# Scores of the stick-breaking and memory heads from 64 rows each, in place of zero-padded 128 rows

## The chip, the cores and the metric

One core of one Trainium2 chip runs the whole program: two blocks of a transformer on 512 tokens of 1024 features. The metric is the device time of one execution in microseconds (us), the median over several runs. The engines are named as the profile names them: PE (TensorE, matrix products), PEld (its weight loads), DVE (VectorE), ACT (ScalarE), POOL (GpSimd) and SP (SyncE, which issues most DMAs).

## The reference, cut to what matters

The first block mixes three kinds of heads (8 stick-breaking heads, 4 heads of a gated recurrence called HGRN, 4 memory heads), adds the result to `x`, and then runs a mixture of experts (PEER). The second block has dilated-window heads and again 4 memory heads. All heads that matter here have 64 features.

```python
def stick_breaking_attention(q, k, v):
    ...
        z = jnp.einsum('bhqd,bhkd->bhqk', q_blk, kh).astype(jnp.float32) * scale
        mask = key_pos[None, :] < q_pos[:, None]
        log_1m = jnp.where(mask, jax.nn.log_sigmoid(-z), 0.0)
        tail = lax.cumsum(log_1m, axis=3, reverse=True) - log_1m
        log_a = jax.nn.log_sigmoid(z) + tail
        a = jnp.where(mask, jnp.exp(log_a), 0.0)
        return jnp.einsum('bhqk,bhkd->bhqd', a.astype(vh.dtype), vh)
...
def memory_attention(q, mem_k, mem_v, q_gain, k_gain):
    qn = rms_norm(q, q_gain)
    kn = rms_norm(mem_k, k_gain)
    logits = jnp.einsum('bshd,bmhd->bhsm', qn, kn).astype(jnp.float32) * scale
    p = jax.nn.softmax(logits, axis=-1)
    return jnp.einsum('bhsm,bmhd->bshd', p.astype(mem_v.dtype), mem_v)
```

The scores `z` and `logits` are sums over only 64 features per head.

## The kernel before, in words

The code is a Tile program: the author writes operations on tiles of named pools, and a scheduler sets the order in which each engine gets its instructions. A pool with two buffers under one name hands them out in the order in which the code asks for them, so the third tile of that name waits until the first is free.

**First block, mixer.** `feat` and `tok` project the normalised tokens with a slab of weights (`mm_feat`, L115 to L123, with 128x512 results; `mm_tok`, L125 to L133, with 128x256 results). Each weight slab is loaded by SP and split into a high part by ACT (L107) and a low part by POOL (L108). These projections depend on little and serve as filler on PE between the pieces of the head computations. The calls at L563 to L582 set the priority: `stick_in(0)`, `stick(0)`, `hgrn_in(0)`, `hgrn(0)`, `stick_in(1)`, `hgrn(1)`, `stick(1)`, `hgrn_in(1)`, `hgrn(2)`, `hgrn(3)`, then `tok` 11 and 12, `mem_q`, `mem_kv`, `mem_out`. After them come `hgrn_out`, the transposes of the mixed rows and the output projection.

**Heads in pairs.** 128 partitions hold the features of two heads: the lower head in rows 0 to 63, the upper one in rows 64 to 127. The queries are kept twice, once with the upper rows zero and once with the lower rows zero (`zero_pads`, L235 to L238, sets the zeros; `padded`, L228 to L233, writes the two halves), so that a product over all 128 rows gives the scores of one head.

**`stick`** (L281) handles four heads at once. For every block of 128 queries (`qb`) it goes through the key blocks `kb` from `qb` down to 0, ten pairs of blocks in all. For each pair:

```python
pz = psa.tile([P, 512], F32, name="att")
for i in range(2):
    nc.tensor.matmul(pz[:, i * 256:(i + 1) * 256], kT[:, i, kb * P:(kb + 1) * P],
                     qz[:, i, :, qb * P:(qb + 1) * P], start=True, stop=True)
z = pool.tile([P, 512], F32, name="sb_a", bufs=4)
...
pc = psa.tile([P, 512], F32, name="att")
```

Both `pz` (scores) and `pc` (cumulative sums) come from `att`, which has two PSUM banks in the first block. DVE copies `pz` to `z` (L297, L299), three ACT passes and one DVE pass make a softplus (L301 to L304), ACT and DVE split it (`sh` L307, `sl` L308), PE sums it into `pc` (L310 with `sh`, L311 with `sl`, L313 with those of earlier blocks), DVE subtracts (L315), ACT takes the exponential (L316). At the end of a query block PE multiplies with the values (L321).

**`hgrn_head`** (L328) runs one recurrence head through eight rounds of DVE, ACT, DVE, PE (scores, L346) and DVE, and ends with the products at L384 to L388.

**`mem_attn`** (L240) serves both blocks: per 128 tokens four score products of 128x256 (L250), two in a bank; maximum (L253), exponentials (L258), transposes (L268), values (L276). In the second block `fill` puts projections between its pieces, and it takes its queries from the tile `dw_qz`, which the window heads use before it (`featT(9, qz, 0.125)`, L1028).

Products with f32 operands appear in the trace as two records (a weight load and a product each) per instruction; products with fp32r operands as one.

Of the kernel before, what the change touches and what calls it, by code (L numbers as in the profile page):

```python
# [84 lines left out]
class Body:  # L85
# [154 lines left out]
    def mem_attn(self, qz, kT, v, emit, pool, psa, pst, psm, scale, fill=None):  # L240

        nc = self.nc
        for b in range(NB):
            p = [pool.tile([P, 2, 256], F32, name="ma_a", bufs=2) for _ in range(2)]
            sm = pool.tile([P, 4], F32, name="ma_sm", bufs=2)
            mx = pool.tile([P, 4], F32, name="ma_mx", bufs=2)
            for c in range(2):
                ps = psa.tile([P, 512], F32, name="att")
                for j in range(2):
                    nc.tensor.matmul(ps[:, j * 256:(j + 1) * 256], qz[:, c, j, b * P:(b + 1) * P], kT[:, c, :],  # L250
                                     start=True, stop=True)
                m = mx[:, 2 * c:2 * c + 2]
                nc.vector.tensor_reduce(m, ps.rearrange("p (j m) -> p j m", j=2), axis=AX.X, op=OP.max, negate=True)  # L253
                if scale != 1.0:
                    nc.vector.tensor_scalar(m, m, scale, None, op0=OP.mult)
                for j in range(2):
                    h = 2 * c + j
                    nc.scalar.activation(p[c][:, j, :], ps[:, j * 256:(j + 1) * 256], AF.Exp, bias=mx[:, h:h + 1],  # L258
                                         scale=scale, accum_out=sm[:, h:h + 1])
# [21 lines left out]
    def stick(self, g, qz, kT, v, mixed, pool, psa, pso):  # L281

        nc = self.nc
        bc = lambda m: m[:, None, :].to_broadcast([P, 4, P])
        v4 = lambda t: t.rearrange("p (h q) -> p h q", h=4)
        for qb in range(NB):
            po = pso.tile([P, 512], F32, name="acc")
            at, parts = {}, []
            for kb in range(qb, -1, -1):
                pz = psa.tile([P, 512], F32, name="att")  # L290
                for i in range(2):
                    nc.tensor.matmul(pz[:, i * 256:(i + 1) * 256], kT[:, i, kb * P:(kb + 1) * P],
                                     qz[:, i, :, qb * P:(qb + 1) * P], start=True, stop=True)

                z = pool.tile([P, 512], F32, name="sb_a", bufs=4)
                if kb == qb:
                    nc.vector.tensor_tensor(v4(z), v4(pz), bc(self.mneg), op=OP.add)  # L297
                else:
                    nc.vector.tensor_copy(z, pz)  # L299
                sp = pool.tile([P, 512], F32, name="sb_sp", bufs=2)  # L300
                nc.scalar.activation(sp, z, AF.Abs)  # L301
                nc.scalar.activation(sp, sp, AF.Exp, scale=-1.0)
                nc.scalar.activation(sp, sp, AF.Ln, bias=1.0)
                nc.vector.scalar_tensor_tensor(sp, z, 0.0, sp, op0=OP.max, op1=OP.add)  # L304
# [10 lines left out]
                nc.vector.tensor_tensor(z, z, pc, op=OP.subtract)  # L315
                nc.scalar.activation(z, z, AF.Exp)  # L316
                at[kb] = z
            for h in range(4):
                c = h // 2
                for kb in range(qb, -1, -1):  # L320
                    nc.tensor.matmul(po[:, h * P:(h + 1) * P], at[kb][:, h * P:(h + 1) * P],  # L321
                                     v[:, kb, c * P:(c + 1) * P], start=kb == qb, stop=kb == 0)
# [105 lines left out]
    def first(self, cp, gp, xr):  # L428
        nc, tc, A = self.nc, self.tc, self.A
        with ExitStack() as es:  # L430
# [84 lines left out]
            def stick_in(eng, g):  # L515
                qz = tp.tile([P, 2, 2, S], F32, name="sb_qz", bufs=2)
                kT = tp.tile([P, 2, S], F32, name="sb_kT", bufs=2)
                v = tp.tile([P, NB, 256], F32, name="sb_v", bufs=2)
                self.zero_pads(qz, eng)
                feat(g, qz, 0.125)  # L520
                feat(2 + g, kT)
                tok(4 + g, slabs(v))
                return qz, kT, v
# [7 lines left out]
            def mem_q():  # L531
                mqz = tp.tile([P, 2, 2, S], F32, name="sb_qz", bufs=2)
                self.zero_pads(mqz, nc.gpsimd)
# [4 lines left out]
                for c in range(2):  # L538
# [3 lines left out]
                    self.padded(mqz[:, c], ps, self.vec[:, V_MQ:V_MQ + 1])  # L542
# [21 lines left out]
            sb = stick_in(nc.vector, 0)  # L564
# [5 lines left out]
            sb = stick_in(nc.gpsimd, 1)  # L570
# [329 lines left out]
    def second(self):  # L900
        nc, tc, A = self.nc, self.tc, self.A
        with ExitStack() as es:
# [125 lines left out]
            featT(9, qz, 0.125)  # L1028
# [28 lines left out]
            self.mem_attn(qz, kTm, vm, emit, pool, psa, pst, psm, 1.0, fill)  # L1057
# [113 lines left out]
```

## Time and profile before

| what | value |
|---|---|
| median of 3 runs | 2064.39 us (2060.55 to 2064.94) |
| the profiled execution, its own time | 2068.49 us |
| its span in the profile | 2066.7 us |
| PE busy | 1940.7 us, 94% of the span |
| DVE busy | 1428.8 us, 69% |
| ACT busy | 886.0 us, 43% |
| POOL busy | 639.8 us, 31% |
| score products of `stick` (L292) | 80 records, 21.8 us busy |
| score products of `mem_attn` (L250), first and second block | 32 and 32 records, 9.9 and 8.6 us busy |

Read it by stages: the mixer of the first block runs from 0 to about 405 us, the experts to about 1750 us, the second block to the end. Busy times of PE overlap, since products are pipelined: the time from the start of one record to the start of the next tells what a record costs, and it is shorter than its duration.

### The profile page before, as it was taken

To read this page: it belongs to the slowest core of one execution; us is meant where nothing else is said; L and a number is where in the kernel's file an instruction comes from. 1 tells how busy PE (TensorE), PEld (TensorE's weight loads), DVE (VectorE), ACT (ScalarE), POOL (GpSimd) and SP (SyncE) were. 2 spreads that over 40 slices of the span, in tenths; PEclk is the share of its full clock that TensorE was granted. 3 is DMA by queue.
4 is the path that set the end of the run, shared out by engine and by line. 5 is a ranking of instruction groups with operands and counts; after the bars stand their busy time and mean duration, and the time that the engine had idled before them with its cause. 6 is when DMAs were issued, how large, how long until landed. Compare 5 with 4: busy or idle time off the path is not lost.

```text
span 2066.7 us, 30059 instructions
## 1 busy us (share of the span) xinstructions
PE 1940.7 (94%) x11393; PEld 1760.8 (85%) x11393; DVE 1428.8 (69%) x2662; ACT 886.0 (43%) x1373; POOL 639.8 (31%) x459
## 2 busy tenths in 40 slices
PE   7999988998779999999999999999999999999998
PEld 6778777998779899899999999999999777779998
DVE  3486976379998866778777777877778675443563
ACT  4564745254437666333333333333333334343352
POOL 4334233075452230144333434343333341000000
PEclk9999999999899999999999999999999999999999
DMA  4211014354224445999888988988988775342211
GB/s 163 69 62 50 33 42 143 123 164 133 92 92 180 177 163 222 313 314 335 304 306 308 316 310 284 337 315 302 313 297 291 272 270 196 103 136 74 82 62 52
DMA packets 150354, 402.90 MB, mean 195 GB/s; under 512 B 11584, under 2 KB 60736, under 8 KB 147008
## 3 DMA queue, kind: packets, MB, share of 16 engines
q1 hardware_dynamic: 112768, 264.64, 38.2%
q0 software_dynamic: 36864, 134.23, 18.0%
q8 instruction: 89, 1.46, 0.3%
q10 hardware_dynamic: 576, 2.10, 0.3%
q14 instruction: 57, 0.47, 0.1%
HBM read 371.05 MB, written 29.88 MB: 194 GB/s over the span
## 4 chain that ended last, share of the span: by engine, by line
PE 59%; DVE 12%; DMA 5%; issue 3%; POOL 1%; ACT 1%; DVEq 0%; POOLq 0%; ACTq 0%
PE o L679 21%; PE hp L634 7%; PE hp L633 7%; PE hp L632 7%; DMA g_row<-peer_v,idx 3%; PE mm L121 2%; PE mm L122 2%; PE mm L123 2%; PE mm L133 2%; PE mm L132 2%; PE mm L131 2%; DVE gated L854 1%; PE g L860 1%; PE mm L861 1%; PE g L861 1%
## 5 line engine op out<-in xcount | busy, mean ns | idle before, releaser
L107 ACT ACTIVATE w_hi<-w_raw 128x1024 fp32r<-128x1024 f32 x366 | 385.8, 1059 | 576.5 <-PE hp L633 168.8
L108 DVE TENSOR_TENSOR w_lo<-w_raw,w_hi 128x1024 fp32r<-128x1024 f32 x268 | 326.3, 1219 | 101.2 <-ACT w_hi L107 100.8
L632 PE MATMUL hp<-xT_hi,w_hi 128*128 128x384 f32 x1024 | 350.5, 342 | 20.9 <-ACT act L636 20.9
L633 PE MATMUL hp<-xT_lo,w_hi 128*128 128x384 f32 x1024 | 349.3, 341 | 0.0
L634 PE MATMUL hp<-xT_hi,w_lo 128*128 128x384 f32 x1024 | 348.8, 341 | 0.0
L108 POOL TENSOR_TENSOR w_lo<-w_raw,w_hi 128x1024 fp32r<-128x1024 f32 x98 | 244.9, 2508 | 254.0 <-ACT w_hi L107 244.7
L885 POOL DMA_INDIRECT g_row<-peer_u,idx x128 | 170.5, 1332 | 353.5 <-PE o L679 128.9
L885 POOL DMA_INDIRECT g_row<-peer_v,idx x128 | 167.5, 1308 | 266.4 <-PE o L679 139.8
L679 PE MATMUL o<-w_hi,wl 128*128 128x512 f32 x768 | 239.8, 394 | 6.4 <-DVE wl L674 6.4
L679 PE MATMUL o<-w_hi,wh 128*128 128x512 f32 x768 | 240.2, 394 | 2.5 <-ACT wh L673 2.5
L679 PE MATMUL o<-w_lo,wh 128*128 128x512 f32 x768 | 238.9, 392 | 0.0
L889 DVE SCALAR_TENSOR_TENSOR g_row<-g_row,kv 128x1024 f32<-128x1024 f32 x128 | 156.3, 1223 | 95.7 <-DMA g_row<-peer_u,idx 94.9
L632 PEld LDWEIGHTS hp<-xT_hi,w_hi 128*128 128x128 f32 x1024 | 196.1, 191 | 25.1 <-ACT act L636 21.5
L633 PEld LDWEIGHTS hp<-xT_lo,w_hi 128*128 128x128 f32 x1024 | 196.2, 192 | 3.6
L634 PEld LDWEIGHTS hp<-xT_hi,w_lo 128*128 128x128 f32 x1024 | 195.6, 191 | 0.0
L894 DVE SCALAR_TENSOR_TENSOR x<-g_row,dots,x 128x1024 f32<-128x1024 f32 x103 | 132.2, 1284 | 81.3 <-DMA g_row<-peer_v,idx 80.6
L679 PEld LDWEIGHTS o<-w_hi,wl 128*128 128x128 f32 x768 | 144.8, 189 | 39.3 <-DVE wl L674 8.3
L679 PEld LDWEIGHTS o<-w_lo,wh 128*128 128x128 f32 x768 | 145.2, 189 | 32.4
L673 ACT ACTIVATE wh<-act 128x384 fp32r<-128x384 f32 x128 | 67.1, 524 | 243.1 <-PE o L679 234.3
L679 PEld LDWEIGHTS o<-w_hi,wh 128*128 128x128 f32 x768 | 143.9, 189 | 27.1 <-ACT wh L673 2.8
L94 POOL TENSOR_TENSOR rs<-rs_t,mhalf 128x1 f32<-128x1 f32 x20 | 13.8, 688 | 391.2 <-DVE rs_t L93 382.0
L121 PE MATMUL mm<-xT_hi,w_hi 128*128 128x256 f32 (+1 forms) x384 | 128.9, 336 | 0.6 <-ACT xT_hi L158 0.6
(335 smaller groups left out, 4013.7 us busy)
## 6 DMA issues: line engine op xcount, KB each, us to landing
w_raw<-peer_uT SPq DMA_DIRECT2D x128, 512.0 KB
w_raw<-peer_v SPq DMA_DIRECT2D x128, 512.0 KB
w_raw<-w_in SPq DMA_DIRECT2D x54, 512.0 KB
gd<-stage SPq DMA_DIRECT2D x24, 1024.0 KB
gt<-gd SPq DMA_DIRECT2D x16, 1536.0 KB
w_raw<-w_query SPq DMA_DIRECT2D x32, 512.0 KB
w_raw<-w_out SPq DMA_DIRECT2D x16, 512.0 KB
b<-c_b SPq DMA_DIRECT2D x16, 448.0 KB
```

What stands on the lines that cost most here:

```text
L107: nc.scalar.activation(hi[:, sl], raw, AF.Copy)
L108: eng.tensor_tensor(lo[:, sl], raw, hi[:, sl].bitcast(F32), op=OP.subtract)
L121: nc.tensor.matmul(ps, a, xh[:, kc, :], start=kc == 0, stop=False)
L122: nc.tensor.matmul(ps, a, xl[:, kc, :], start=False, stop=False)
L632: nc.tensor.matmul(ps, uh[:, kc, :], hi[:, kc, P:], start=kc == 0, stop=False)
L633: nc.tensor.matmul(ps, uh[:, kc, :], lo[:, kc, P:], start=False, stop=False)
L634: nc.tensor.matmul(ps, ul[:, kc, :], hi[:, kc, P:], start=False, stop=kc == KC - 1)
L673: nc.scalar.activation(wh, w, AF.Copy)
L679: last = nc.tensor.matmul(out[b][n], s_[:, sl], m_[:, n * 512:(n + 1) * 512], start=i == 0 and m_ is vh and s_ is wh, stop=i == NE - 1 and ...
L885: dma = nc.gpsimd.indirect_dma_start(out=u, out_offset=None, in_=A["peer_v" if k >= P else "peer_u"], in_offset=bass.IndirectOffsetOnAxis( ...
L889: nc.vector.scalar_tensor_tensor(u, u, 1.0, self.h2, op0=OP.mult, op1=OP.mult, accum_out=dots[:, c:c + 1])
L894: nc.vector.scalar_tensor_tensor(y, u, dots[:, c:c + 1], x, op0=OP.mult, op1=OP.add)
```

## The change

The queries are kept once, without zeros (`zero_pads` and `padded` are no longer called for `stick` and for the memory heads of the first block; the second block's memory heads get an own tile `dw_mq`). A score product takes the 64 rows of one head. `j` is 0 for the lower and 1 for the upper head; the scores of all lower heads go to one bank, those of all upper heads to another. In `stick` one bank holds the scores of two key blocks, so two key blocks are started at once, and the copy to `z` takes two instructions for each key block in place of one.

```diff
-    def mem_attn(self, qz, kT, v, emit, pool, psa, pst, psm, scale, fill=None):
+    def mem_attn(self, q, kT, v, emit, pool, psa, pst, psm, scale, fill=None):
...
+            ps = [psa.tile([P, 512], F32, name="att").rearrange("p (c m) -> p c m", c=2) for _ in range(2)]
             for c in range(2):
-                ps = psa.tile([P, 512], F32, name="att")
                 for j in range(2):
-                    nc.tensor.matmul(ps[:, j * 256:(j + 1) * 256], qz[:, c, j, b * P:(b + 1) * P], kT[:, c, :],
-                                     start=True, stop=True)
-                m = mx[:, 2 * c:2 * c + 2]
-                nc.vector.tensor_reduce(m, ps.rearrange("p (j m) -> p j m", j=2), axis=AX.X, op=OP.max, negate=True)
+                    r = slice(64 * j, 64 * j + 64)
+                    nc.tensor.matmul(ps[j][:, c], q[r, c, b * P:(b + 1) * P], kT[r, c, :], start=True, stop=True)
+            for j in range(2):
+                nc.vector.tensor_reduce(mx[:, j], ps[j], axis=AX.X, op=OP.max, negate=True)
...
-    def stick(self, g, qz, kT, v, mixed, pool, psa, pso):
+    def stick(self, g, q, kT, v, mixed, pool, psa, pso):
...
             for kb in range(qb, -1, -1):
-                pz = psa.tile([P, 512], F32, name="att")
-                for i in range(2):
-                    nc.tensor.matmul(pz[:, i * 256:(i + 1) * 256], kT[:, i, kb * P:(kb + 1) * P],
-                                     qz[:, i, :, qb * P:(qb + 1) * P], start=True, stop=True)
-
-                z = pool.tile([P, 512], F32, name="sb_a", bufs=4)
-                if kb == qb:
-                    nc.vector.tensor_tensor(v4(z), v4(pz), bc(self.mneg), op=OP.add)
-                else:
-                    nc.vector.tensor_copy(z, pz)
+                if (qb - kb) % 2 == 0:
+
+                    two = range(kb, max(kb - 2, -1), -1)
+                    for k in two:
+                        z[k] = pool.tile([P, 512], F32, name="sb_a", bufs=4)
+                    pz = [psa.tile([P, 512], F32, name="att").rearrange("p (n i q) -> p n i q", n=2, i=2) for _ in range(2)]
+                    for n, k in enumerate(two):
+                        for i in range(2):
+                            for j in range(2):
+                                r = slice(64 * j, 64 * j + 64)
+                                nc.tensor.matmul(pz[j][:, n, i], kT[r, i, k * P:(k + 1) * P], q[r, i, qb * P:(qb + 1) * P],
+                                                 start=True, stop=True)
+                    for n, k in enumerate(two):
+                        for j in range(2):
+
+                            d = z[k].rearrange("p (i j q) -> p j i q", i=2, j=2)[:, j]
+                            if k == qb:
+                                nc.vector.tensor_tensor(d, pz[j][:, n], self.mneg[:, None, :].to_broadcast([P, 2, P]), op=OP.add)
+                            else:
+                                nc.vector.tensor_copy(d, pz[j][:, n])
...
-                    if len(dst.shape) == 4:
-                        self.padded(dst[:, c], ps, scale)
-                    else:
-                        nc.scalar.activation(dst[:, c], ps, AF.Copy, scale=scale)
+                    nc.scalar.activation(dst[:, c], ps, AF.Copy, scale=scale)
...
-            def stick_in(eng, g):
-                qz = tp.tile([P, 2, 2, S], F32, name="sb_qz", bufs=2)
+            def stick_in(g):
+                q = tp.tile([P, 2, 2, S], F32, name="sb_qz", bufs=2)[:, 0]
...
-                self.zero_pads(qz, eng)
-                feat(g, qz, 0.125)
+                feat(g, q, 0.125)
...
-                    self.padded(mqz[:, c], ps, self.vec[:, V_MQ:V_MQ + 1])
+                    nc.scalar.activation(mqz[:, c], ps, AF.Copy, scale=self.vec[:, V_MQ:V_MQ + 1])
...
-            sb = stick_in(nc.vector, 0)
+            sb = stick_in(0)
...
-            featT(9, qz, 0.125)
+            mq = pool.tile([P, 2, S], F32, name="dw_mq")
+            featT(9, mq, 0.125)
...
-            self.mem_attn(qz, kTm, vm, emit, pool, psa, pst, psm, 1.0, fill)
+            self.mem_attn(mq, kTm, vm, emit, pool, psa, pst, psm, 1.0, fill)
```

The order that the scheduler makes of it differs in two stretches: the mixer of the first block, and the memory heads of the second. Between them every engine gets the same instructions in the same order. (From the change on, L292 is L299, L310, L311 and L313 are L319, L320 and L322, L321 is L329, L346 is L354, and L376 is L384.)

On PE, the start of `stick(0)`. The number behind `att` tells the PSUM tile; projections are left out at the lines of dots. Before:

```order
L292 MATMUL att_581<-sb_qz_317,sb_kT_318 128x256 x2
...
L310 MATMUL att_595<-sb_h_591,tri_564 128x512
L292 MATMUL att_614<-sb_qz_317,sb_kT_318 128x256
L311 MATMUL att_595<-sb_l_592,tri_564 128x512
...
L310 MATMUL att_628<-sb_h_624,tri_564 128x512
L292 MATMUL att_633<-sb_qz_317,sb_kT_318 128x256
L311 MATMUL att_628<-sb_l_625,tri_564 128x512
```

Now (578 and 616 are tiles of the lower heads, 579 and 617 of the upper ones):

```order
L299 MATMUL att_578<-sb_qz_317,sb_kT_318 128x128
L299 MATMUL att_579<-sb_qz_317,sb_kT_318 128x128
L299 MATMUL att_578<-sb_qz_317,sb_kT_318 128x128
L299 MATMUL att_579<-sb_qz_317,sb_kT_318 128x128
...
L319 MATMUL att_595<-sb_h_591,tri_560 128x512
L299 MATMUL att_616<-sb_qz_317,sb_kT_318 128x128 x3
L320 MATMUL att_595<-sb_l_592,tri_560 128x512
L299 MATMUL att_616<-sb_qz_317,sb_kT_318 128x128
...
L299 MATMUL att_617<-sb_qz_317,sb_kT_318 128x128 x3
L329 MATMUL acc_576<-sb_v_319,sb_a_577 128x128 x4
L299 MATMUL att_617<-sb_qz_317,sb_kT_318 128x128
```

Lower and upper heads alternate in the first run of score products; in the second query block the products of the lower heads come as a run of their own, and those of the upper heads later.

On PE, the end of `stick(1)` (its last value products are the x13) and the start of `hgrn(3)` (its first products read `hg_qf`). Before:

```order
L376 MATMUL tp<-cst,hg_kt 128x128 x3
...
L346 MATMUL hs<-hg_qf 128x128 x2
L384 MATMUL hs<-hg_st,hg_qt 128x128
L385 MATMUL hs<-hg_i,hg_sc 128x128
L346 MATMUL hs<-hg_qf 128x128 x2
...
L310 MATMUL att<-sb_h,tri 128x512
...
L321 MATMUL acc<-sb_v,sb_a 128x128 x13
```

Now:

```order
L329 MATMUL acc<-sb_v,sb_a 128x128 x13
L384 MATMUL tp<-cst,hg_kt 128x128 x3
L393 MATMUL hs<-hg_i,hg_sc 128x128
...
L392 MATMUL hs<-hg_st,hg_qt 128x128
L393 MATMUL hs<-hg_i,hg_sc 128x128
...
L354 MATMUL hs<-hg_qf 128x128 x4
```

`hgrn(3)` now begins behind the whole of `stick(1)`; 89 of the projections of 128x256 follow its start up to the first transposes of `mem_q`, where 132 did.

On PE, one block of tokens of the second block's memory heads; again the number behind `att` tells the tile. Before:

```order
L250 MATMUL att_17949<-kv_15048,dw_qz_16038 128x256
L276 MATMUL mm_17933<-kv_15048,ma_sp_17919 128x128
L250 MATMUL att_17949<-kv_15048,dw_qz_16038 128x256
L276 MATMUL mm_17933<-kv_15048,ma_sp_17920 128x128
...
L250 MATMUL att_17955<-kv_15048,dw_qz_16038 128x256 x2
```

Now:

```order
L252 MATMUL att_17929<-kv_15100,dw_mq_17591 128x256
L252 MATMUL att_17930<-kv_15100,dw_mq_17591 128x256
L277 MATMUL mm_17913<-kv_15100,ma_sp_17899 128x128
L277 MATMUL mm_17913<-kv_15100,ma_sp_17900 128x128
...
L252 MATMUL att_17929<-kv_15100,dw_mq_17591 128x256
L252 MATMUL att_17930<-kv_15100,dw_mq_17591 128x256
```

The four products stand in two runs, each of one lower and one upper head.

## Rows read from the trace of the kernel before

**Rows 1.** The page, busy time, share of the span and instructions of each engine.

```profile
PE 1940.7 (94%) x11393; PEld 1760.8 (85%) x11393; DVE 1428.8 (69%) x2662; ACT 886.0 (43%) x1373; POOL 639.8 (31%) x459
```

**Rows 2.** Busy time by stretch: length, PE, PEld, DVE, ACT, POOL, granted clock, DMA.

```profile
60.00:210.00 150.00, 139.12 (x794) 116.55 (x793) 100.38 (x188) 84.58 (x137) 52.70 (x52) 0.99 0.20 63
...
189.00:262.00 73.00, 66.50 (x407) 57.00 (x406) 62.00 (x130) 49.26 (x81) 17.98 (x23) 1.00 0.09 30
...
300.00:345.00 45.00, 35.73 (x233) 32.71 (x234) 24.98 (x55) 23.11 (x49) 18.06 (x13) 0.85 0.30 103
1975.00:2004.00 29.00, 29.00 (x219) 27.08 (x219) 15.88 (x34) 14.18 (x43) 0.00 (x0) 1.00 0.12 38
```

**Rows 3.** Timeline of PE in stick(0): start, length, line, operation, [idle before <-releaser].

```profile
66.33 0.28 PE L133 MATMUL mm<-w_hi,xT_lo 128*128 128x256 f32 x1
66.45 0.28 PE L131 MATMUL mm<-w_hi,xT_hi 128*128 128x256 f32 x1
...
66.81 1.03 PE L292 MATMUL att<-sb_qz,sb_kT 128*128 128x256 f32 x4
67.48 0.58 PE L121 MATMUL mm<-xT_hi,w_hi 128*128 128x512 f32 x1
67.90 0.39 PE L122 MATMUL mm<-xT_lo,w_hi 128*128 128x512 f32 x1
68.14 0.39 PE L123 MATMUL mm<-xT_hi,w_lo 128*128 128x512 f32 x1
...
74.21 0.50 PE L310 MATMUL att<-sb_h,tri 128*128 128x512 f32 x1 [1.71 <-ACT sb_h L307]
...
90.44 0.50 PE L311 MATMUL att<-sb_l,tri 128*128 128x512 f32 x1 [1.47 <-DVE sb_l L308]
...
141.39 0.50 PE L310 MATMUL att<-sb_h,tri 128*128 128x512 f32 x1
```

**Rows 4.** Timeline of PE: products of 128 columns, f16 (gates) and f32 (L321).

```profile
699.72 0.30 PE L861 MATMUL g<-gated,onehot 128*128 128x128 f16 x1
699.84 0.30 PE L860 MATMUL g<-gated,onehot 128*128 128x128 f16 x1
...
261.50 3.11 PE L321 MATMUL acc<-sb_v,sb_a 128*128 128x128 f32 x26
```

**Rows 5.** Timeline of PE: score products of the second block's memory heads.

```profile
1975.77 1.89 PE L250 MATMUL att<-kv,dw_qz 128*128 128x256 f32 x8
```

**Rows 6.** DVE by line and shape, 60 to 300 us: busy, mean ns.

```profile
L299 DVE COPY sb_a<-att 128x512 f32<-128x512 f32 x12 | 8.2, 685 | 0.2
...
L325 DVE TENSOR_TENSOR xrow<-acc,hr_r 128x256 f32<-128x256 f32 x8 | 3.4, 425 | 6.1 <-POOL hr_r L94 6.1
```

**Rows 7.** Timeline of PE: first and last products of hgrn(1), then of hgrn(3).

```profile
170.21 1.06 PE L346 MATMUL hs<-hg_qf 128*128 128x128 f32 x8
195.38 0.39 PE L385 MATMUL hs<-hg_i,hg_sc 128*128 128x128 f32 x2
...
255.40 0.71 PE L346 MATMUL hs<-hg_qf 128*128 128x128 f32 x4
290.18 0.39 PE L385 MATMUL hs<-hg_i,hg_sc 128*128 128x128 f32 x2
```

**Rows 8.** Timeline of the start, DVE, POOL and PE.

```profile
13.71 0.91 DVE L238 MEMSET sb_qz<- 64x1024 f32 x1 [0.15 <-issue]
...
14.15 2.34 POOL L108 TENSOR_TENSOR w_lo<-w_raw,w_hi 128x1024 fp32r<-128x1024 f32 x1
...
14.55 2.50 DVE L168 TENSOR_SCALAR xrow<-sb_qz,rs 128x1024 f32<-128x1024 f32 x1
...
17.10 0.47 PE L143 MATMUL att<-cst,xrow 128*128 128x128 f32 x1 [2.43 <-DVE xrow L168]
```

**Rows 9.** ACT, the padded evictions: duration min/median/max in ns, first and last start.

```profile
L233 ACT ACTIVATE sb_qz<-mm x8: 578/592/597, 38.6 to 141.8; 64x512 f32<-64x512 f32 x8
L233 ACT ACTIVATE sb_qz<-tp,vec x4: 682/682/682, 302.3 to 306.7; 64x512 f32<-64x512 f32 x4
```

More of the change, by code (lines that the diff above doesn't have):

```diff
@@ L245, in mem_attn @@
             sm = pool.tile([P, 4], F32, name="ma_sm", bufs=2)
-            mx = pool.tile([P, 4], F32, name="ma_mx", bufs=2)
+            mx = pool.tile([P, 2, 2], F32, name="ma_mx", bufs=2)
+            ps = [psa.tile([P, 512], F32, name="att").rearrange("p (c m) -> p c m", c=2) for _ in range(2)]
             for c in range(2):
-                ps = psa.tile([P, 512], F32, name="att")
                 for j in range(2):
-                    nc.tensor.matmul(ps[:, j * 256:(j + 1) * 256], qz[:, c, j, b * P:(b + 1) * P], kT[:, c, :],
-                                     start=True, stop=True)
-                m = mx[:, 2 * c:2 * c + 2]
-                nc.vector.tensor_reduce(m, ps.rearrange("p (j m) -> p j m", j=2), axis=AX.X, op=OP.max, negate=True)
+                    r = slice(64 * j, 64 * j + 64)
+                    nc.tensor.matmul(ps[j][:, c], q[r, c, b * P:(b + 1) * P], kT[r, c, :], start=True, stop=True)
+            for j in range(2):
+                nc.vector.tensor_reduce(mx[:, j], ps[j], axis=AX.X, op=OP.max, negate=True)
                 if scale != 1.0:
-                    nc.vector.tensor_scalar(m, m, scale, None, op0=OP.mult)
-                for j in range(2):
+                    nc.vector.tensor_scalar(mx[:, j], mx[:, j], scale, None, op0=OP.mult)
+                for c in range(2):
                     h = 2 * c + j
-                    nc.scalar.activation(p[c][:, j, :], ps[:, j * 256:(j + 1) * 256], AF.Exp, bias=mx[:, h:h + 1],
+                    nc.scalar.activation(p[c][:, j, :], ps[j][:, c], AF.Exp, bias=mx[:, j, c:c + 1],
                                          scale=scale, accum_out=sm[:, h:h + 1])
@@ L278, in mem_attn @@
             emit(b, own(po), rs)
[L281 removed]
+    def stick(self, g, q, kT, v, mixed, pool, psa, pso):
         nc = self.nc
[L284 to L285 removed]
         for qb in range(NB):
             po = pso.tile([P, 512], F32, name="acc")
[L288 removed]
+            parts, z = [], {}
             for kb in range(qb, -1, -1):
[L290 to L299 removed]
+                if (qb - kb) % 2 == 0:
[16 more added lines that the diff above has]
+                                nc.vector.tensor_copy(d, pz[j][:, n])
@@ L300, in stick @@
                 sp = pool.tile([P, 512], F32, name="sb_sp", bufs=2)
-                nc.scalar.activation(sp, z, AF.Abs)
+                nc.scalar.activation(sp, z[kb], AF.Abs)
                 nc.scalar.activation(sp, sp, AF.Exp, scale=-1.0)
                 nc.scalar.activation(sp, sp, AF.Ln, bias=1.0)
-                nc.vector.scalar_tensor_tensor(sp, z, 0.0, sp, op0=OP.max, op1=OP.add)
+                nc.vector.scalar_tensor_tensor(sp, z[kb], 0.0, sp, op0=OP.max, op1=OP.add)
                 sh = pool.tile([P, 512], F32R, name="sb_h", bufs=4)
@@ L314, in stick @@
                 parts += [sh, sl]
-                nc.vector.tensor_tensor(z, z, pc, op=OP.subtract)
-                nc.scalar.activation(z, z, AF.Exp)
-                at[kb] = z
+                nc.vector.tensor_tensor(z[kb], z[kb], pc, op=OP.subtract)
+                nc.scalar.activation(z[kb], z[kb], AF.Exp)
             for h in range(4):
@@ L320, in stick @@
                 for kb in range(qb, -1, -1):
-                    nc.tensor.matmul(po[:, h * P:(h + 1) * P], at[kb][:, h * P:(h + 1) * P],
+                    nc.tensor.matmul(po[:, h * P:(h + 1) * P], z[kb][:, h * P:(h + 1) * P],
                                      v[:, kb, c * P:(c + 1) * P], start=kb == qb, stop=kb == 0)
@@ L531, in mem_q @@
             def mem_q():
-                mqz = tp.tile([P, 2, 2, S], F32, name="sb_qz", bufs=2)
-                self.zero_pads(mqz, nc.gpsimd)
+                mqz = tp.tile([P, 2, 2, S], F32, name="sb_qz", bufs=2)[:, 0]
                 for b in range(NB):
@@ L569, in first @@
             hgrn(0, *hin)
-            sb = stick_in(nc.gpsimd, 1)
+            sb = stick_in(1)
             hgrn(1, *hin)
```

2 lines of the change are left out of this document (1 added, 1 removed).

## The prediction

> **What bounds the kernel now.** I read the page first: PE is busy for 94% of the span [rows 1], so the question is always whether PE, or something that PE waits for, ends last in the stretch that the change touches. The chain of waits, read next, follows the loop over the experts and the second block; before 405 us it is broken off, so for the mixer I went by the stretches of busy time and by PE's timeline. From 60 to 210 us PE has 139 us of work in 150 [rows 2]: it is the bound there. From 189 to 262 us, where `stick(1)` and `hgrn(2)` run beside each other, PE leaves 6.5 us of 73 idle and DVE works 62 [rows 2]: the two share the bound. From 300 to 345 us PE idles for 9 us and its granted clock falls to 0.85. At the second block's memory heads PE is busy without a gap [rows 2].
>
> A median of this kernel can be told from no change from about 0.2% on, which is 4.1 us.
>
> **What a score product costs.** Records are priced from start to start. Four records of 128x256 f32 take 1.03 us [rows 3] and eight take 1.89 us [rows 5]: 0.215 us each. Eight records of 128x128 f32 take 1.06 us [rows 7] and 26 take 3.11 us [rows 4]: 0.114 us each. f16 records of 128 columns start 0.12 us apart [rows 4], and so do fp32r records of twice the columns [rows 3]. So about 0.114 us looks like the least distance of two records, whatever they stream.
>
> *Stick.* Before: 40 products of 256 columns, 80 records, 80 x 0.215 = 17.2 us. Now: 80 products of 128 columns, 160 records. If none overlaps they take 160 x 0.114 = 18.2 us, 1.0 us more. Two products can overlap only where a lower and an upper head follow each other. Counted over the whole order, the 80 products stand in 30 runs, and only three of them alternate over four products; nearly all others are of one half alone, since the bank of the upper heads becomes free later than that of the lower ones (the first place of the order shows both kinds). In an alternating run of four, the eight records come as two of one half, then two of the other, and so on; if the second record of one half runs beside the first of the next, five steps are left of eight. Three runs save 3 x 3 x 0.114 = 1.0 us. Net 0.0 us. No row shows a product of 64 rows, so the bounds are +1.0 us (no overlap) and 18.2/2 - 17.2 = -8.1 us (everything overlaps); I take the value that counts the runs.
>
> *Memory heads.* The products keep 256 columns, 32 records per block at 0.215 us, 6.9 us each. First block: two alternating runs of four among eight runs, 6 steps x 0.215 = -1.3 us. Second block: one run of four and four runs of one lower and one upper head (the third place of the order), 3 + 4 steps, -1.5 us; PE has no gap there, so all of it counts. Bounds: 0 and -3.4 us for each block.
>
> The Trainium skill (TensorEngine Tiling, Overview) promises up to a factor of two for products over 64 rows, as independent tiles. By that rule the stick term would be at its bound of -8.1 us and both memory terms at -3.4 us; the sum goes by the runs.
>
> **Copies on DVE.** A copy of 128x512 from PSUM takes 685 ns; an operation of 128x256 on PSUM takes 425 ns [rows 6]. Two in place of one add 2 x 425 - 685 = 165 ns to each of 20 pairs of blocks. Those of `stick(0)` lie beside PE-bound work and cost nothing while PE has projections to do. Those of `stick(1)` lie where DVE is at 62 of 73 us: 10 x 0.165 = +1.6 us (bounds 0 and +3.3).
>
> **Order.** In `stick` the next scores were issued only about when the sums of the block before were: ten turns from 74.21 to 141.39 us, 67.2/9 = 7.5 us each [rows 3]. Now two key blocks start together and go through ACT and DVE one behind the other, so `stick` ends earlier among its neighbours. The second place of the order shows what that does: `hgrn(3)` starts behind all of `stick(1)`. Before, `hgrn(3)` ran 35.2 us from first to last product, `hgrn(1)`, which has no stick beside it, 25.6 us [rows 7]. The chain gets up to 9.6 us shorter. But more PE work stands ahead of it: 8 sums at 0.24 us (the step from L122 to L123) [rows 3], 26 value records at 0.114 us, and 132 - 89 = 43 projections at 0.12 us [rows 3, 4], together 1.9 + 3.0 + 5.2 = 10.1 us. What of it fits into the 6.5 us in which PE idled is free. So the term is +0.5 us if nothing fits and -6.0 us if 6.5 us do. DVE is nearly full there, so I take the middle, -2.7 us.
>
> **Start.** DVE's two fills (0.91 us each) stand between the scalings of the first rows. The last scaling starts at 14.55 us and takes 2.50 us because POOL's split has begun at 14.15 us; PE waits 2.43 us for it [rows 8]. Without the fills that scaling comes up to 0.9 us earlier, still beside a POOL split: -0.9 us (bounds 0 and -2.4).
>
> **What costs nothing.** The padded evictions fall from eight of 592 ns to four of about the same length, and from four of 682 ns to two, on ACT [rows 9]. The first lie in a PE-bound stretch; the second come before `mem_kv`, whose keys the memory heads need as well and later. If that cover were gone the gain would be 1.4 us. POOL's fills go too; POOL works 53 of 150 us [rows 2]. On SP the reload of `x` moves ahead of two constants that are read after the output projection; nothing that is needed sooner stands behind it.
>
> **Sum.** 0.0 - 1.3 - 1.5 + 1.6 - 2.7 - 0.9 = -4.8 us. Against the profiled execution's own 2068.5 us this gives 2063.7 us; that execution lay 4.1 us above the median of 2064.4 us, so for the median I forecast 2059.6 us.
>
> **Rivals.**
>
> *Slower: a price for going from 128 rows to 64 and back.* If PE must empty itself before a product of another row count may start, each run pays on entering and on leaving. A record of 0.30 us whose successor starts after 0.12 us has 0.18 us in flight [rows 4]; that is the most a switch could expose. 30 + 17 = 47 runs make 94 switches, 94 x 0.18 = +16.9 us, and with the sum +12.1 us: 2076.5 us. It decides for slower from (4.8 + 4.1)/94 = 0.095 us a switch on. For it: the runs are short and scattered between projections. Against it: part of the runs lies where DVE is the bound, and a change from f32 to fp32r products costs nothing that shows (66.81 to 67.90 us is 1.09 us for four records at 0.215 us and one at 0.24 us [rows 3]), though both are over 128 rows. The Trainium skill states such a rule (TensorEngine Tiling, Key Properties): a change of the tiling mode drains the engine. No row here can show it.
>
> *No change: no overlap, and DVE sets the order's term.* Alternating halves run one after the other: +1.0 us for stick, 0 for the memory heads; `hgrn(3)` +0.5, copies +1.6, start -0.9: +2.2 us, 2066.6 us. For it: the distance of 0.114 us between any two records. This is also the case in which the change does not do what it says.
>
> *Much faster: the stick's turns were the hidden bound.* `hgrn(3)` takes its full -6.0 us, the copies are hidden, and the two waits of 1.71 and 1.47 us in `stick(0)` go: -0.9 - 6.0 - 2.8 - 3.2 = -12.9 us, 2051.5 us. Against it: 62 of 73 us on DVE.
>
> **How the numbers follow.** Forecast 0.45: its value lies just past the bound of 4.1 us, so I give 0.31 of it to faster and 0.14 to no change. Much faster 0.11. No change 0.17. Switches 0.27, of which 0.23 slower and 0.04, with a small price, no change. Faster 0.31 + 0.11 = 0.42, same 0.14 + 0.17 + 0.04 = 0.35, slower 0.23. The range from 2052 to 2073 us takes in the forecast's bounds, the no-change case and switches up to (4.8 + 8.6)/94 = 0.14 us; about one in ten is left out above it and a little less below. The forecast's own range is 2055 to 2064 us.
>
> **What would show it.** Right: in the first run of scores, records of the two halves start closer than 0.114 us, and the second block's stretch from the first memory score to the last gets 1.5 us shorter; `hgrn(3)` takes about 26 us; the scaling L168 of the last rows ends before 16.5 us. Wrong: the product that follows a score run starts 0.1 us or more late at every run (switches); scores of the two halves 0.114 us apart everywhere (no overlap); PE's idle time between 189 us and the end of `stick(1)` as large as now while DVE is full (order).

## The result and the profile after

The change made the kernel slower: 2093.15 us median of three runs (2085.07, 2093.15, 2098.13) against 2062.47 us (the median of the three runs of the table and one more), a ratio of 1.0143 (95% interval 1.0100 to 1.0187). A fourth run took 2707.74 us at a mean granted clock of 0.651 and is left out. The forecast was 2059.6 us, with a range up to 2073.

PE's line of the page, where [rows 1] showed 1940.7 us:

```profile
PE 1962.6 (94%) x11473; PEld 1771.0 (85%) x11473; DVE 1423.6 (68%) x2680; ACT 877.9 (42%) x1365; POOL 634.0 (30%) x455
```

Busy time by stretch of the changed kernel (columns as in [rows 2]); the first four stretches answer to [rows 2], the second block's one being moved by 16 us:

```profile
60.00:210.00 150.00, 142.49 (x814) 118.59 (x814) 95.32 (x195) 76.54 (x126) 49.03 (x50) 0.95 0.18 57
189.00:262.00 73.00, 65.44 (x363) 52.88 (x361) 52.24 (x101) 40.93 (x68) 16.60 (x20) 0.93 0.09 30
300.00:345.00 45.00, 33.60 (x237) 29.96 (x235) 25.71 (x60) 21.03 (x38) 21.03 (x16) 0.89 0.19 58
1991.00:2020.00 29.00, 28.57 (x211) 23.99 (x210) 15.38 (x33) 13.55 (x43) 0.00 (x0) 1.00 0.11 37
75.00:80.00 5.00, 5.00 (x17) 3.44 (x17) 1.45 (x3) 0.63 (x1) 0.00 (x0) 0.58 0.13 51
80.00:85.00 5.00, 5.00 (x16) 4.07 (x16) 1.39 (x5) 1.75 (x4) 1.01 (x1) 0.50 0.00 0
242.00:246.00 4.00, 4.00 (x18) 3.55 (x18) 2.26 (x6) 0.63 (x1) 0.56 (x2) 0.50 0.01 4
```

The third number from the right is the granted clock. It was 0.99 and 1.00 in the first two stretches before; now it is 0.95 and 0.93, and for whole pieces of `stick` it is 0.50, which is 1.2 GHz of 2.4. PE looks fuller (142 us of 150), but with slower records. Before, DVE worked 62 us between 189 and 262 us; now it works 52, although `stick(1)` ends 14 us behind that window. So DVE is less full there than it was.

PE's timeline shows how one such piece begins:

```profile
74.06 0.50 PE L319 MATMUL att<-sb_h,tri 128*128 128x512 f32 x1 [1.95 <-ACT sb_h L316]
74.49 0.93 PE L299 MATMUL att<-sb_qz,sb_kT 64*128 64x128 f32 x6
75.35 0.50 PE L320 MATMUL att<-sb_l,tri 128*128 128x512 f32 x1
75.78 0.79 PE L299 MATMUL att<-sb_qz,sb_kT 64*128 64x128 f32 x2
...
78.07 1.65 PE L299 MATMUL att<-sb_qz,sb_kT 64*128 64x128 f32 x6
79.65 2.07 PE L329 MATMUL acc<-sb_v,sb_a 128*128 128x128 f32 x8
...
85.53 0.63 PE L123 MATMUL mm<-xT_hi,w_lo 128*128 128x512 f32 x1
86.24 0.40 PE L122 MATMUL mm<-xT_lo,w_hi 128*128 128x512 f32 x1
```

A wait of 1.95 us, then score products of one half alone, and everything up to 85.9 us takes about double. In the kernel before a wait of 1.71 us stood at the same place [rows 3], and nothing slowed down. That such a wait and such products always bring the clock down does not follow: the `stick`-only kernel below has both, at full clock.

Where the time went, from PE's timelines (us from the start; one profiled execution each). The last three kernels are explained below.

| | before | changed | two key blocks | changed, 128 rows | in turns |
|---|---|---|---|---|---|
| the profiled execution's own time | 2068.5 | 2085.1 | 2071.8 | 2080.6 | 2072.5 |
| first score of `stick(0)` | 66.8 | 66.8 | 67.5 | 67.8 | 67.9 |
| end of `stick(1)`'s value products | 264.6 | 275.8 | 262.6 | 262.6 | 275.7 |
| `hgrn(2)`, first product | 221.6 | 230.1 | 233.5 | 221.6 | 227.7 |
| `hgrn(2)`, last product starts | 256.2 | 281.8 | 269.0 | 269 | 276 |
| `hgrn(3)`, first and last product | 255.4, 290.2 | 284.3, 311.9 | 271.1, 298 | 271, 299 | 276, 303 |
| first transpose of `mem_q` | 294.2 | 313.9 | 303.2 | 300.7 | 303.2 |
| first block's memory scores, first and last | 320.3, 356.1 | 341.9, 382.0 | 329.0, 365.2 | 328.6, 364.4 | 326.8, 368.9 |
| end of PE's work | 2058.4 | 2074.7 | 2061.7 | 2070.2 | 2062.3 |

The changed kernel has lost 20 us when `mem_q` begins and 26 us at the last memory score. At the end the two profiled executions differ by 16 us only. Part of that lies in before's execution, which is 4 to 6 us above the medians of that kernel and in which PE works 149 us of the stretch from 1600 to 1760 us, where the changed kernel's PE works 157. Part lies in the changed kernel's execution, which is 4 to 8 us below the medians of that kernel. The execution of the 128-row kernel, on the other hand, lies 7.6 us above its median (2073.0 us), so the ends of the columns are no measure of the kernels; the medians below are.

### The profile page after: what moved, and what is told of

Same layout as the page of the kernel before. It is cut to its first block, busy times and chain, and to the rows that moved or that the text cites. A ratio compares the mean times of both kernels' runs of the same rounds, so it can differ in the third digit from the quotient of the medians.

```text
span 2083.3 us, 30226 instructions
## 1 busy us (share of the span) xinstructions
PE 1962.6 (94%) x11473; PEld 1771.0 (85%) x11473; DVE 1423.6 (68%) x2680; ACT 877.9 (42%) x1365; POOL 634.0 (30%) x455
## 3 DMA queue, kind: packets, MB, share of 16 engines
q0 software_dynamic: 36864, 134.23, 17.7%
## 4 chain that ended last, share of the span: by engine, by line
PE 52%; DVE 12%; DMA 9%; issue 4%; POOL 1%; ACT 1%; DVEq 0%; POOLq 0%; ACTq 0%
PE o L682 19%; DMA g_row<-peer_v,idx 6%; PE hp L637 6%; PE hp L636 6%; PE hp L635 5%; PE mm L131 2%; PE mm L133 2%; PE mm L121 2%; PE mm L132 2%; PE mm L122 2%; PE mm L123 2%; DVE x L897 1%; DVE gated L857 1%; PE g L863 1%; PE mm L864 1%
## 5 line engine op out<-in xcount | busy, mean ns | idle before, releaser
L888 POOL DMA_INDIRECT g_row<-peer_v,idx x128 | 162.4, 1269 | 268.2 <-PE o L682 143.9
```

Of the source, the lines that this page charges most:

```text
L888: dma = nc.gpsimd.indirect_dma_start(out=u, out_offset=None, in_=A["peer_v" if k >= P else "peer_u"], in_offset=bass.IndirectOffsetOnAxis( ...
```

## The experiments

My theory ahead of the runs: in `stick`, products over 64 rows let the clock fall behind waits (A). The rivals: the order with two key blocks at a time (B), and a price for going to 64 rows and back (C), which was the prediction's slower rival. Each median stands beside runs of the kernel before on the same chip (medians 2061.1, 2062.3 and 2061.8 us in the three groups of runs). "Lost to the clock" is 1 minus the mean granted clock, times the time, as a median over all timed runs: the most that the lower level can have cost, since PE also waits in such stretches.

| kernel | median us | ratio to before, 95% | lost to the clock, us (range) |
|---|---|---|---|
| before | 2061 to 2062 | | 54 (51 runs) |
| changed, again | 2089.0 | 1.0139, 1.0122 to 1.0156 | 69 (67 to 73) |
| changed, 128 rows | 2073.0 | 1.0054, 1.0034 to 1.0074 | 57 (54 to 62) |
| `stick` only | 2084.1 | 1.0109, 1.0086 to 1.0132 | 65 (60 to 71) |
| memory heads only | 2068.4 | 1.0042, 1.0023 to 1.0061 | 58 (54 to 67) |
| memory heads only, 128 rows | 2066.2 | 1.0011, 0.9998 to 1.0024 | 56 (52 to 62) |
| memory heads in whole runs | 2081.2 | 1.0082, 1.0063 to 1.0102 | 65 (60 to 67) |
| two key blocks | 2071.5 | 1.0031, 1.0015 to 1.0047 | 57 (54 to 62) |
| changed, in turns | 2073.3 | 1.0050, 1.0029 to 1.0070 | 60 (54 to 66) |
| in turns, 128 rows | 2065.8 | 1.0012, 0.9994 to 1.0031 | 58 (52 to 62) |
| one more product an expert, 128 rows | 2087.3 | 1.0113, 1.0083 to 1.0144 | 50 (46 to 52) |
| the same over 64 rows | 2125.1 | 1.0286, 1.0255 to 1.0317 | 46 (42 to 49) |

### The changed kernel again, and with 128 rows

```diff
-                                r = slice(64 * j, 64 * j + 64)
+                                r = slice(0, P)
```

The same line is changed in `stick` and in `mem_attn`, and nothing else. The scores of two heads are then summed, so this kernel leaves out their separation.

> The changed kernel once more, beside the next three, so that all stand on one chip. Any theory: 2085 to 2098 us, 1.0 to 1.9% above the kernel before; granted clock below 0.9 somewhere in 75 to 90 us and in 238 to 270 us.

> Every score product of the changed kernel over all 128 rows again (the unpadded queries and keys of both heads, so it sums the scores of the two heads); every engine gets the same instructions in the same order. Theory A (products over 64 rows let the granted clock fall): the clock is back at 1.0 in 75 to 90 us and 238 to 255 us, and some 20 us of the loss go: 2062 to 2075 us, within 0.6% of the kernel before. Theory B (the order, with two key blocks at a time, makes the waits after which the clock falls): no change against the changed kernel within 0.3%, 2085 to 2098 us, and the clock falls in the same places. Theory C (a price for switching between 128 and 64 rows, 94 times): 9 to 17 us less than the changed kernel, with the clock still low in the places of the waits.

Measured: 2089.0 and 2073.0 us. So 16 us of the 28 us loss belong to the 64 rows, and 12 us to the rest of the change. PE's order is the same in both, so A and B are both half right. C's 9 to 17 us take in the 16 us as well: this pair alone does not tell a price for switching from the clock. The clock with 128 rows, same columns:

```profile
75.00:80.00 5.00, 4.76 (x23) 4.34 (x24) 2.05 (x4) 0.82 (x2) 0.00 (x0) 0.66 0.31 102
80.00:85.00 5.00, 5.00 (x28) 4.18 (x27) 1.92 (x6) 3.95 (x8) 1.01 (x1) 1.00 0.00 0
242.00:246.00 4.00, 3.81 (x26) 3.52 (x27) 4.00 (x8) 1.30 (x3) 0.59 (x2) 1.00 0.00 0
189.00:262.00 73.00, 64.53 (x400) 56.61 (x399) 57.07 (x111) 43.04 (x72) 16.67 (x20) 0.93 0.09 30
```

The clock falls behind the wait here too, but is at 1.00 again from 80 us on, where the changed kernel stays at 0.50 beyond 85. From 189 to 262 us both have a mean of 0.93: here the low pieces only lie elsewhere. Over all runs the changed kernel loses 67 to 73 us to the clock and this one 54 to 62: the ranges don't touch.

### Half of the change each

`stick` new and the memory heads padded, and the other way round; the functions are taken unchanged from the two kernels.

> Only stick from 64 rows, the memory heads of both blocks padded as before. Theories A and B: the loss sits in stick, so it stays: 2082 to 2098 us. If the memory heads (clock 0.83 in 340 to 380 us) carried it: 2062 to 2075 us.

> Only the memory heads from 64 rows, stick as before. Theories A and B: 2056 to 2066 us, since PE does not wait long around them. If the memory heads carried the loss: 2080 us or more.

Measured: 2084.1 us (+23.0) and 2068.4 us (+7.3). The two add up to 30 where the whole change costs 28. Most of the loss sits in `stick`, as expected; but the memory heads were expected at 2066 us at most and are a loss of their own.

The profile of the `stick`-only kernel has a wait as long and the same products of one half at the place where the clock fell in the changed kernel. PE's timeline, then the busy time by stretch:

```profile
74.21 0.49 PE L319 MATMUL att<-sb_h,tri 128*128 128x512 f32 x1 [1.94 <-ACT sb_h L316]
74.64 0.93 PE L299 MATMUL att<-sb_qz,sb_kT 64*128 64x128 f32 x6
```

```profile
75.00:80.00 5.00, 5.00 (x30) 3.70 (x29) 1.64 (x4) 1.02 (x2) 0.00 (x0) 1.00 0.19 68
80.00:85.00 5.00, 5.00 (x23) 3.89 (x21) 2.60 (x8) 4.40 (x9) 1.02 (x1) 1.00 0.01 2
```

The clock stays at 1.00 here, while both profiled executions of the changed kernel fall to 0.58 and 0.55 between 75 and 80 us. So theory A says too much of this place: behind the wait the clock can fall, and need not. What is measured is the sum over the whole runs, 65 us lost in place of 54.

### What a visit to 64 rows costs

To the kernel before I added one f32 product of 128x128 behind the first products of each of the 128 experts, where PE does not wait, once over 128 and once over 64 rows; its result is not used.

```diff
-                ps = psh.tile([P, 512], F32, name="hp")[:, :TD]
+                hp = psh.tile([P, 512], F32, name="hp")
+                ps = hp[:, :TD]
...
+                nc.tensor.matmul(hp[:, TD:], self.ident[:64], self.ident[:64], start=True, stop=True)
```

> The kernel before with one more f32 product of 128x128 over 128 rows for each of the 128 experts, behind the first products of the expert, where PE is full and its clock is at 1.0. The product's result is not used. Two records at 0.114 us and up to 0.19 us on the way back to fp32r products make 29 to 53 us: 2090 to 2114 us.

> The same with the added product over 64 rows; every engine has the same instructions in the same order. If going to 64 rows and back has a price of 0.29 us a run (the second block's memory heads show 0.45 us more for a block with three runs although 1.72 us of score products become 1.29): 128 x 0.29 = 37 us more than with 128 rows. If only the clock behind waits matters: the same time as with 128 rows within 4 us, as PE does not wait here.

Measured: 2087.3 and 2125.1 us. The 128 rows cost a little less than expected; the difference of 37.8 us is the 37 us expected, 0.295 us a visit on average. Where PE is full it is more: from the 40th to the 120th added product the lag of the second timeline grows from 5.4 to 36.4 us, 0.39 us a visit. The first 32 products lie before 820 us, where PE idles for a tenth of the time. PE's timeline, first over 128, then over 64 rows:

```profile
1102.94 0.34 PE L635 MATMUL hp<-xT_hi,w_lo 128*128 128x384 f32 x1
1103.11 0.38 PE L636 MATMUL hp<-cst 128*128 128x128 f32 x2
1103.25 0.71 PE L681 MATMUL o<-w_hi,wh 128*128 128x512 f32 x2
```

```profile
1100.54 0.34 PE L635 MATMUL hp<-xT_hi,w_lo 128*128 128x384 f32 x1
1100.80 0.48 PE L636 MATMUL hp<-cst 64*128 64x128 f32 x2
1101.22 0.73 PE L681 MATMUL o<-w_hi,wh 128*128 128x512 f32 x2
```

The 64-row product starts 0.26 us after its predecessor in place of 0.17, and what follows it starts 0.42 us later in place of 0.14. These visits did not lower the clock: 46 us are lost to it, fewer than with 128 rows. So C is shown as a price of its own. The Trainium skill (TensorEngine Tiling (Array Packing), Key Properties) says that a change of tiling mode drains the engine; these rows agree, with a delay on the way in and a longer one on the way out.

### What overlaps

Two runs of four products in the changed kernel, the first with the halves alternating, the second of one half:

```profile
66.75 0.72 PE L299 MATMUL att<-sb_qz,sb_kT 64*128 64x128 f32 x8
67.39 0.50 PE L121 MATMUL mm<-xT_hi,w_hi 128*128 128x512 f32 x1
...
91.69 1.16 PE L299 MATMUL att<-sb_qz,sb_kT 64*128 64x128 f32 x8
92.77 0.49 PE L329 MATMUL acc<-sb_v,sb_a 128*128 128x128 f32 x2
```

From the first record to what follows: 0.64 us alternating, 1.08 us for one half. Over 128 rows, in the same order, these two runs take 0.80 and 0.96 us. So I held the products in turns by a chain of order-only dependencies, upper head first, in `stick` and the memory heads, and ran that order over 64 and over 128 rows (summing two heads again).

```diff
-                            for j in range(2):
+                            for j in (1, 0):
...
-                                nc.tensor.matmul(pz[j][:, n, i], ...
+                                last = self.behind(last, nc.tensor.matmul(pz[j][:, n, i], ...
```

> The changed kernel with the score products of stick and of the memory heads held in turns (upper, lower, upper, lower), so that nearly all runs of two and more products alternate; about as many runs (54) as in the changed kernel. If alternating halves run two at a time and same-half runs do not, some 50 of the 80 products of stick save 0.12 us each, up to 6 us: 2081 to 2087 us. If the price of a run and the clock carry the loss, no change that can be measured: 2085 to 2093 us.

> The kernel with the heads in turns (2073 us), its score products over all 128 rows, in the same order on every engine (scores of two heads summed). If halves in turns make 64 rows neutral (what the pairs save pays for the visits): 2069 to 2077 us, the rest being the order. If the visits are still unpaid there (46 at 0.295 us): 2058 to 2066 us.

Measured: 2073.3 us, below both ranges that I had set down, and 16 us less than the changed kernel with the same number of visits (47 in each trace). With 128 rows in this order 2065.8 us: the 64 rows still cost 7.5 us, so the visits are not paid for even in turns: the second of the two cases that I had set down, with 7.5 us in place of 13.6 left unpaid.

The two pairs together tell what the turns changed. The price of the 64 rows fell from 16 to 7.5 us, and the loss that the order has over 128 rows fell from 12 to 4 us (an interval that takes in none); each of these is known to some 5 us only. So about half of the 16 us has nothing to do with 64 rows, and why this order is cheaper is not shown. The other half goes with the clock and with the score records. Lost to the clock are 60 us in turns and 58 over 128 rows in the same order, where it was 69 and 57. Summed from the start of each run of `stick`'s scores to the start of what follows, without waits, in one profile each: 14.9 us before, 25.5 changed, 17.6 in turns; over 128 rows 18.3 and 17.7.

### Two key blocks at a time

The kernel before, padded, with one part of the change: the scores of two key blocks are issued together, each with a bank and one copy.

```diff
-                pz = psa.tile([P, 512], F32, name="att")
+                if (qb - kb) % 2 == 0:
+                    two = range(kb, max(kb - 2, -1), -1)
+                    pz = [psa.tile([P, 512], F32, name="att") for _ in two]
...
```

> The kernel before with one part of the change: stick issues the scores of two key blocks together (padded, 256 columns, a bank and one copy for each key block). The kernel over 128 rows of the first call kept 0.54% of the loss. If working on two key blocks at a time is what cost that: 2067 to 2075 us, hgrn(2) takes over 40 us from its first to its last product (34 before) and the transposes of mem_q begin 4 us or more later than before. If the split copies on DVE did it: within 0.2% of the kernel before, 2057 to 2065 us.

Measured: 2071.5 us, +9.3 us by the medians (the ratio, 1.0015 to 1.0047, makes 3 to 10 us), which cannot be told from the 12 us of the 128-row kernel. PE's timeline, first and last product of `hgrn(2)`, first of `hgrn(3)`:

```profile
233.47 1.05 PE L349 MATMUL hs<-hg_qf 128*128 128x128 f32 x8
...
268.97 0.39 PE L388 MATMUL hs<-hg_i,hg_sc 128*128 128x128 f32 x2
271.08 1.16 PE L349 MATMUL hs<-hg_qf 128*128 128x128 f32 x8
```

`hgrn(2)` is not longer, as I had expected (36 us for 35), but starts 11 us later than before and ends 13 us later. `stick(1)` ends 2 us earlier and `hgrn(3)` takes 27 us in place of 35, and yet `mem_q` begins 9 us later. Six of the 11 us are there before `stick(1)`: `hgrn(0)` begins at 111.5 us in place of 105.5, and `hgrn(1)` at 176.2 in place of 170.2 [rows 7].

The size is that of the 12 us, the path is another. In the order of the 128-row kernel `hgrn(2)` begins as early as before and takes 47 us in place of 35, and in turns over 128 rows, with two key blocks at a time as well, the loss is 4 us. So two key blocks at a time can cost 9 us; that they are what costs most of the 12 us is not shown.

### The memory heads

First the memory-only kernel with 128 rows in the same order (the diff of the first experiment, in `mem_attn` alone). Then the memory-only kernel with the four products of a block kept together in turns behind the value products of the block before (`last = nc.tensor.matmul(po[...` carries the chain on).

> The kernel of the first call that has only the memory heads from 64 rows (it took 0.42% more than the kernel before), now with its score products over all 128 rows and the same order on every engine (the scores of two heads are summed). If the 64 rows cost it: within 0.2% of the kernel before, 2058 to 2066 us, and the second block's stretch from first to last score at 23.9 us in place of 24.4. If the new order of the memory heads costs it: 2066 to 2072 us.

> Only the memory heads from 64 rows, and the four score products of a block of tokens kept together in turns (upper, lower, upper, lower) behind the value products of the block before: 8 visits to 64 rows in place of some 18. A visit at 0.295 us and pairs at 0.43 us make 1.16 us a block in place of 1.72 us, 0.57 us less: the second block's stretch takes 21.6 us (to 23.3 us if PE then waits 0.4 us in each block for the exponentials). Whole kernel 2056 to 2064 us, if the clock stays up in the first block's memory heads; 2065 us or more if it falls there as long as with the memory heads alone (13 us at half).

Measured with 128 rows: 2066.2 us, +0.11% by the ratio, with an interval that takes in none (+4.4 us by the medians); with 64 rows +0.42%. The second block's scores, from the first record to the last, take 24.2 us, over 64 rows 24.7, before 24.0. PE's timeline of one block of tokens in the second block, first over 128, then over 64 rows:

```profile
1986.12 1.03 PE L269 MATMUL tp<-cst,ma_a 128*128 128x128 f32 x8
1986.99 0.60 PE L252 MATMUL att<-kv,dw_mq 128*128 128x256 f32 x2
1987.42 0.47 PE L277 MATMUL mm<-kv,ma_sp 128*128 128x128 f32 x2
1987.72 0.60 PE L252 MATMUL att<-kv,dw_mq 128*128 128x256 f32 x2
1988.27 1.83 PE L277 MATMUL mm<-kv,ma_sp 128*128 128x128 f32 x14
1989.93 1.03 PE L252 MATMUL att<-kv,dw_mq 128*128 128x256 f32 x4
...
1990.92 0.27 PE L132 MATMUL mm<-w_lo,yT_hi 128*128 128x256 f32 x1
```

```profile
1986.77 1.03 PE L269 MATMUL tp<-cst,ma_a 128*128 128x128 f32 x8
1987.74 0.70 PE L252 MATMUL att<-kv,dw_mq 64*128 64x256 f32 x2
1988.36 0.49 PE L277 MATMUL mm<-kv,ma_sp 128*128 128x128 f32 x2
1988.78 0.70 PE L252 MATMUL att<-kv,dw_mq 64*128 64x256 f32 x2
1989.41 1.83 PE L277 MATMUL mm<-kv,ma_sp 128*128 128x128 f32 x14
1991.16 0.70 PE L252 MATMUL att<-kv,dw_mq 64*128 64x256 f32 x4
...
1992.02 0.28 PE L132 MATMUL mm<-w_lo,yT_hi 128*128 128x256 f32 x1
```

The same instructions take 4.80 and 5.25 us. Over 64 rows a pair of lower and upper (x4) takes 0.64 us to what follows, a single product (x2) 0.62: the second half is free, and each visit pays. With pairs at 0.43 us the scores save 0.43 us a block; that the block still takes 0.45 us more puts a visit at (0.43 + 0.45)/3 = 0.29 us here, by estimate. The Trainium skill (TensorEngine Tiling (Array Packing), Overview) promises up to a factor of two; the pairs reach it, the visits take it back.

The whole runs came out at 2081.2 us, 12.7 us worse than the memory-only kernel and far above the 2056 to 2064 us that I had set down for a clock that stays up. The runs did cost what I worked out (1.06 us from the first record to what follows, and some 0.1 us ahead of it). But the scores now wait for the values of the block before, and PE for what comes behind them:

```profile
PE hs L143 <- DVE sb_kT L168: 5.7, 1, 5.7
PE tp L540 <- DVE xrow L536: 4.8, 1, 4.8
PE tp L268 <- ACT ma_a L258: 4.3, 2, 2.2
PE tp L268 <- ACT ma_sp L272: 2.1, 3, 0.7
```

That is the view of waits from 300 to 400 us (total, times, longest). The first stands where the memory-only kernel waits 4.7 us for its first exponentials, and the second (4.8 us) it has as well. The last two, 6.4 us for the exponentials and for copies of their transposes, all lie behind 350 us, where the memory-only kernel has 0.5 us of them. And the clock falls behind them, as the same stretch of the memory-only kernel and of this one tells:

```profile
360.00:380.00 20.00, 19.86 (x159) 18.57 (x158) 8.68 (x17) 6.12 (x15) 0.00 (x0) 1.00 0.43 166
360.00:380.00 20.00, 13.95 (x66) 10.87 (x63) 5.15 (x13) 5.05 (x18) 0.00 (x0) 0.66 0.31 105
```

From the first record of the first block's memory scores to the last it takes 50.5 us, in the memory-only kernel 39.8 and before 35.8; in the second block 24.7, 24.7 and 24.0 us. So most of the loss lies in the first block; how it divides between the waits and the clock is not shown.

## Why the prediction was wrong, point by point

- **What bounds the kernel.** Right for `stick(0)` and the second block. In `stick(1)` I took DVE and PE to share the bound; DVE works 10 us less from 189 to 262 us now, and `stick(1)` ends 11 us later.
- **Stick, 0.0 us.** The step that failed most. That only runs of alternating halves overlap was right. The term had no price for the visits, which stood in a rival: 30 visits at 0.29 to 0.39 us make 9 to 12 us. And it took the clock as given at 1.0. The score records themselves went from 14.9 to 25.5 us, about 3 us of it through records at half clock. Of these 10.6 us, 3.4 are there over 128 rows already (18.3 us): the step from 40 products of 256 columns to 80 of 128, which I had put at 1.0 us.
- **Memory heads, -1.3 and -1.5 us.** The overlap is as forecast, the visits eat it: a block with one pair and two single products takes 0.45 us more where the pair should have saved 0.2, and the second block's stretch from first to last score 24.7 us in place of 24.0. In the memory-only kernel the scores of the first block spread over 39.8 us in place of 35.8 (35.8 with 128 rows).
- **Copies, +1.6 us.** An operation on a half takes 416 to 424 ns as assumed from [rows 6]. The 128-row kernel, which has the split copies, and the one with two key blocks, which has not, differ by 1.5 us (2073.0 and 2071.5): no contradiction, but within the noise.
- **Order, -2.7 us (+0.5 to -6.0).** Wrong in sign, the second step that failed. `hgrn(3)` takes some 27 us as forecast, but `stick(1)` ends 11 us later in the changed kernel (2 us earlier over 128 rows and with two key blocks alone). I did not ask what becomes of `hgrn(2)`, which shares DVE and ACT with `stick(1)`: it ends 12 to 13 us later over 128 rows and with two key blocks alone, 26 us later in the changed kernel. With 128 rows the whole of the change costs 12 us. Through which wait `hgrn(2)` loses its time is not shown.
- **Start, -0.9 us.** The transposes of the last rows begin 1.67 us earlier (15.43 for 17.10 us in [rows 8]), but the first score starts at 66.75 us for 66.81: the gain is gone before it counts.
- **The rivals.** The slower one came in by its price: 0.29 to 0.39 us a visit is 0.15 to 0.19 us a switch, past the 0.095 us from which it decides; 94 switches make 14 to 18 us, which with -4.8 us is a loss of 9 to 13 us. I gave it 0.27, because going from f32 to fp32r products showed no cost at 128 rows, which says nothing of another row count. It still misses the order and the clock, so the time lies beyond the range.

The balance: the 64 rows cost 16 us where the score terms forecast -2.8 (0.0 - 1.3 - 1.5), and the rest of the change 12 us where copies, order and start forecast -2.0. Some 3 to 6 of the 16 us are the memory heads' (7.3 us in the memory-only kernel less 4.4 with its 128 rows by the medians, 0.42% less 0.11% by the ratios), the others are `stick`'s. Of the 16 the clock accounts for up to 12 us (69 for 57 us lost), the visits and the unpaired halves for the rest. How much of the clock's 12 us lay under other engines' work is not separated, and so the two parts of the 16 us are not settled to the microsecond. What in the new order costs the 12 us stays open: two key blocks at a time cost 9 us in one order, 4 us are left in another.

## What to carry to other kernels

Going to 64-row products and back has a price (0.3 to 0.4 us a visit here), so packing two heads can pay only where lower and upper products alternate in long runs and the scheduler keeps these whole; count visits, not products. In no run here did it beat the padded kernel. Before such a change, ask of each neighbour on the shared engines, not only of the one that moves forward, when it will start. Run the new order with the old products too: here the order alone cost almost as much as the 64 rows. And read the granted clock over many runs, since one profile can show it low at a place where another does not.

## What the runs showed of the hardware

- A visit to 64 rows among products of 128 rows costs 0.39 us with a product of 128 columns and, by estimate, 0.29 us with those of 256, with PE full and the clock at 1.0: the 64-row product starts some 0.1 us later, and what follows it later again.
- Lower and upper 64-row products that alternate overlap (0.64 us for the run of four above, 0.80 over 128 rows), those of one half don't (1.08 and 0.96 us).
- In the same order on every engine, `stick` and memory heads over 64 rows lost 67 to 73 us to the clock and over 128 rows 54 to 62; with the halves in turns, 60 and 58 us at the median. Behind a wait of 1.95 us and products of one half the clock stayed at 1.2 GHz for 10 us in the changed kernel; in the `stick`-only kernel, behind a wait of 1.94 us and the same products, it stayed at 2.4 GHz. What decides was not measured.
